# Hybrid attention layer on one core: block turns behind the weights, low halves on GpSimd, v through DRAM

## The chip, the cores and the metric

The kernel runs on one core of a Trainium2 chip. The core has TensorE (PE in the profile, with its weight loads as PEld), VectorE (DVE), ScalarE (ACT), GpSimd (POOL) and SyncE (SP), which here only issues DMA transfers. The metric is the device time in microseconds of one execution; several executions are timed and their median is given.

## The reference

One layer of an encoder trunk on 1024 frames of width 1024, with 16 meta tokens put ahead of them (1040 positions):

```python
u = rmsnorm(h, norm_g)
proj = einsum('bld,dc->blc', u, w_in)            # 1024 -> 4096 columns
sb_q, sb_k, sb_v, sb_g, df_q, df_k, df_v, df_g = split(proj)
# stick-breaking attention, 8 heads of 64, per block of 128 queries
z = q @ k.T * scale
log_keep = where(strict, log_sigmoid(-z), 0)
stick = reverse exclusive cumsum of log_keep along the keys
w = where(strict, exp(log_sigmoid(z) + stick), 0)
sb_o = w @ v
# differential attention, 4 heads, rotary, chunk-causal mask
a = softmax(s1) - lam * softmax(s2);  df_o = rmsnorm(a @ v) * (1 - lambda_init)
mix = concat([sb_o * silu(sb_g), df_o * silu(df_g)])
y = rmsnorm(h + mix @ w_out)[N_META:]
```

## The kernel before

**Numbers.** All is float32. The projections and q-times-k are done as products of two halves: a high half rounded to the short form in which TensorE is fast (float32r) and a low half that holds the rest. `mm3` (lines 150 to 160) makes three matmuls for each of the 8 slices of the contraction: high x high (L157), high x low (L158) and low x high (L159). `w_half` (line 140) loads half of a unit's weights (four slices of 128x128) from DRAM into `wraw` (L144, two buffers), ScalarE copies it to its high half `wh` (L146), and VectorE takes the difference as its low half `wl` (L147); `wh` and `wl` have three buffers each. There are 58 such halves outside the start: 8 for each of groups 1 to 7, and two for v of group 0.

**Stages.** The work has eight groups: 0 to 3 are pairs of stick-breaking heads (SB), 4 to 7 are heads of differential attention (DF). Each group has four projection units, q, k, v and gate. A weaver alternates the attention of group g with the projections of group g+1, by the costs that each piece states, so that TensorE has projection matmuls while VectorE and ScalarE work on weights. The framework's scheduler then sets the order of the instructions on each engine; each engine works through its own list in order, and so does SP's list of DMA transfers. A wait on one list holds up all that stands behind it there.

**SB attention.** The positions are stored in reverse, so block b of 128 queries has n = 8 - b key tiles behind it: 8, 7, 6, 5, 4, 3, 2, 1. `sb_attention` walks steps s = 0 to 8; step s makes the weights of block s and transposes those of block s-1, for both heads, and after every second block `sb_pv` multiplies the pair (b, b+1). `sb_weights` (line 512) does z on TensorE (L508, L509), a mask on VectorE (L520), two sigmoids on ScalarE (L521, L522), a running product on VectorE (TENSOR_TENSOR_SCAN, L525) and a product of weights (L527); GpSimd copies 16 columns of it aside (L528). The results lie in `be`, which has four buffers.

**Turning the weights.** The product with v needs the weights with keys on the partitions. `sb_transpose` (line 531) has two ways. With n of at least `SB_TURN` = 4 and b even (blocks 0, 2 and 4), and while the two rotary tables `cosr` and `sinr` aren't loaded yet (groups 0 to 2), `turn` (line 251) transposes blocks of 32x32 on VectorE (L256) into one of these two tables' room, writes the result to a scratch in DRAM with four transfers (L260) and reads it back whole (L262), at once, all in the step behind the weights. All other blocks are transposed by TensorE, 128x128 at a time (L551), and copied out of PSUM by ScalarE (L552). The results lie in `wt`, one tile for each head and pair of blocks, with two buffers: the next pair's tile is free when `sb_pv` (L574) has read the last pair's.

**v.** `make_v` (line 264) turns v of groups 1 to 6 in the same manner with VectorE (L279), but brings the pieces to their place with 16 transfers of 32 KB from SBUF to SBUF (L283), with runs of 128 bytes.

Of the kernel before, what the change touches and what calls it, by code (L numbers as in the profile page):

```python
# [52 lines left out]
class Build:  # L53
    def __init__(self, tc, es, i, out, mix_dram, turn_dram):
        self.tc, self.nc, self.es, self.i = tc, tc.nc, es, i
        self.out, self.mix_dram, self.turn_dram = out, mix_dram, turn_dram
        self.n = 0

        self.nu, self.rotary = 0, False

# [79 lines left out]
    def w_half(self, u, h, copy=None, room=None):  # L140
# [5 lines left out]
        (copy or nc.scalar.copy)(out=hi, in_=raw)  # L146
        nc.vector.tensor_sub(lo, raw, hi.bitcast(F32))  # L147
        return hi, lo
# [101 lines left out]

    def turn(self, u, src, dst):


        nc = self.nc
        n = src.shape[1] // P
        nc.vector.transpose(out=u[:, :n * P].rearrange("p (m t r) -> p t m r", m=4, r=32),  # L256
                            in_=src.rearrange("p (t m r) -> p t m r", m=4, r=32))
        d = self.turn_dram[self.nu % 4]
        for a in range(4):
            nc.sync.dma_start(out=d[:, a, :n * 32].rearrange("(m k) c -> k m c", k=32),  # L260
                              in_=u[32 * a:32 * a + 32, :n * P].rearrange("k (m c) -> k m c", m=4))
        nc.sync.dma_start(out=dst, in_=d[:, :, :n * 32].rearrange("p a (t r) -> p a t r", r=32))  # L262

    def make_v(self, t, st, sb, on_pe):
# [12 lines left out]
        else:  # L277
            u = self.tl(self.tp, [P, T], F32, "t")[:, :SEQ]
            nc.vector.transpose(out=u, in_=t[:, off:off + SEQ])  # L279
            u = u.rearrange("p (t j r) -> p t j r", j=4, r=32)  # L280
            for a in range(0, P, 32):
                for j in range(4):
                    nc.sync.dma_start(out=v[32 * j:32 * j + 32, :, a:a + 32], in_=u[a:a + 32, :, j, :])  # L283
        st["v"] = v
# [227 lines left out]
    def sb_weights(self, st, hd, b):  # L512
# [15 lines left out]
        nc.gpsimd.tensor_copy(st["wrem"][32 * hd:32 * hd + 16, b], beta[:16, :16])  # L528
        st["w", hd, b] = beta

    def sb_transpose(self, st, hd, b):
# [8 lines left out]
        wt = st["wt", hd][:, e]  # L540
        if e == 0 and n >= SB_TURN and not self.rotary:
            self.nu += 1
            u = self.tl(self.const, [P, T], F32, ("cosr", "sinr")[self.nu % 2])
            self.turn(u, w[:, NMETA:NMETA + n * P], wt[:, :, e:e + n])
            return
# [367 lines left out]

SB_TURN = 4

# [63 lines left out]
```

## Time and profile before

| what | value |
|---|---|
| median of 3 runs | 689.79 us (686.61 to 689.93) |
| the profiled execution | 689.24 us, span 687.4 us |
| PE busy | 663.5 us (97% of the span) |
| PEld busy | 577.5 us (84%) |
| DVE busy | 513.2 us (75%) |
| ACT busy | 350.8 us (51%) |
| POOL busy | 137.0 us (20%) |
| mean granted TensorE clock | 0.987 of full speed |
| DMA queues of SP | 76,416 packets, 78.10 MB, 41.6% of 16 engines' span |

The span runs from the first to the last instruction that the profile shows. The ends of matmuls are modelled, since they are pipelined: 0.40 us stands for a matmul that the next one follows after 0.23 us, so distances between starts tell more than durations. The granted clock is what the chip's throttle allowed TensorE, as a share of full speed. From its first z (L508) to the sum that ends it (L596), the attention of group 0 lies at 62 to 151 us of the span, of group 1 at 123 to 218, of group 2 at 201 to 292 and of group 3 at 273 to 368 (they overlap, since the next group's first z starts before the last products of the one before); then come the DF groups, and from about 560 us the output projection.

### The profile page before, as it was taken

What the parts mean: (1) busy time and instruction counts of PE and PEld (TensorE: products, weight loads), DVE (VectorE), ACT (ScalarE), POOL (GpSimd) and SP (SyncE); (2) the same over time, 40 slices, a digit from 0 to 9 for tenths busy, and PEclk for the clock granted to TensorE, in tenths of its full rate; (3) what the DMA queues carried; (4) which work ended last, traced back from release to release, by engine and by line L of the source; (5) the groups of instructions that cost most, each with busy time, mean ns of one, the idle gap of its engine ahead of it and who ended that gap; (6) DMA issues with size and microseconds to landing.
All of it is one profiled execution on the core that took longest, in us unless ns stands there. A gap on an engine that the chain in (4) does not pass through costs nothing.

```text
span 687.4 us, 11400 instructions
## 1 busy us (share of the span) xinstructions
PE 663.5 (97%) x3908; PEld 577.5 (84%) x3908; DVE 513.2 (75%) x1053; ACT 350.8 (51%) x931; POOL 137.0 (20%) x188
## 2 busy tenths in 40 slices
PE   8999999999979998989999999999999999999996
PEld 7888998798858996779878998899889987888785
DVE  6744998699829985698858785878589687776653
ACT  6513545545534552565544656555655436655642
POOL 0030021122210112040411022202222053011222
PEclk9999999999989999999999999999999999999998
DMA  8215647374645658022352324042504772122322
GB/s 327 93 33 140 171 124 188 87 218 121 144 118 138 165 112 239 16 77 55 72 123 62 74 67 124 32 117 53 124 32 101 201 239 87 63 84 77 105 92 92
DMA packets 76617, 78.83 MB, mean 115 GB/s; under 512 B 32528, under 2 KB 56208, under 8 KB 76560
## 3 DMA queue, kind: packets, MB, share of 16 engines
q1 hardware_dynamic: 76416, 78.10, 41.6%
q8 instruction: 31, 0.51, 0.3%
q14 instruction: 26, 0.21, 0.1%
q10 hardware_dynamic: 144, 0.00, 0.0%
HBM read 41.44 MB, written 14.42 MB: 81 GB/s over the span
## 4 chain that ended last, share of the span: by engine, by line
PE 71%; DVE 10%; DMA 8%; issue 3%; ACT 3%; SPq 3%; POOL 1%; POOLq 0%; DVEq 0%; ACTq 0%
PE mm L157 12%; PE mm L158 12%; PE mm L159 12%; PE mm L756 10%; PE pv L694 4%; PE z L508 4%; PE z L509 4%; PE pv L574 3%; DVE be L525 2%; PE tr L677 2%; DMA wt<-turn_scratch 2%; PE tr L551 2%; DVE be L527 1%; DMA hb<-ha 1%; SPq L283 1%
## 5 line engine op out<-in xcount | busy, mean ns | idle before, releaser
L157 PE MATMUL mm<-xh,wh 128*128 128x346 f32 (+2 forms) x592 | 211.6, 358 | 2.6 <-DVE be L211 2.2
L158 PE MATMUL mm<-xl,wh 128*128 128x346 f32 (+2 forms) x592 | 210.9, 356 | 0.0
L159 PE MATMUL mm<-xh,wl 128*128 128x346 f32 (+2 forms) x592 | 209.9, 355 | 0.0
L157 PEld LDWEIGHTS mm<-xh,wh 128*128 128x128 f32 x592 | 112.3, 190 | 13.3 <-DVE be L211 2.5
L159 PEld LDWEIGHTS mm<-xh,wl 128*128 128x128 f32 x592 | 112.1, 189 | 9.1 <-issue 0.5
L158 PEld LDWEIGHTS mm<-xl,wh 128*128 128x128 f32 x592 | 112.2, 189 | 8.5 <-issue 0.7
L525 DVE TENSOR_TENSOR_SCAN be<-be,zero 128x1040 f32<-128x1040 f32 (+7 forms) x64 | 92.2, 1446 | 16.5 <-ACT be L521 16.4
L521 ACT ACTIVATE be<-z 128x456 f32<-128x456 f32 (+8 forms) x112 | 49.8, 458 | 86.7 <-DVE z L520 51.2
L643 ACT ACTIVATE be<-z,nm 128x346 f32<-128x346 f32 (+8 forms) x112 | 59.9, 540 | 50.4 <-DVE nm L640 34.6
L528 POOL COPY rem<-be 16x16 f32<-16x16 f32 x64 | 34.6, 540 | 192.0 <-DVE be L527 177.0
L633 DVE TENSOR_REDUCE nm<-z 128x1 f32<-128x346 f32 (+8 forms) x112 | 54.6, 502 | 4.7 <-PE z L509 3.6
L522 ACT ACTIVATE be<-z 128x346 f32<-128x346 f32 (+8 forms) x112 | 48.6, 464 | 13.3 <-DVE be L527 12.1
L146 ACT CAST wh<-wraw 128x512 fp32r<-128x512 f32 x58 | 36.2, 626 | 36.6 <-PE mm L158 27.2
L527 DVE TENSOR_TENSOR be<-be,be 128x1039 f32<-128x1039 f32 (+7 forms) x64 | 49.2, 769 | 4.0 <-ACT be L522 0.9
L147 DVE TENSOR_TENSOR wl<-wraw,wh 128x512 fp32r<-128x512 f32 x58 | 40.0, 691 | 10.3 <-ACT wh L146 9.7
L702 POOL TENSOR_TENSOR rr<-rr,mhalf 128x1 f32<-128x1 f32 x32 | 19.7, 616 | 137.8 <-DVE rr L701 98.9
L508 PE MATMUL z<-ha,qa 128*128 128x346 f32 (+8 forms) x112 | 37.9, 344 | 4.2 <-DMA ha<-ha 1.9
L574 PE MATMUL pv<-wt,v 128*64 128x256 f32 (+1 forms) x336 | 37.4, 368 | 4.6 <-DMA wt<-turn_scratch 4.6
L508 PE MATMUL z<-hb,qb 128*128 128x346 f32 (+8 forms) x112 | 38.2, 341 | 0.6 <-ACT be L522 0.3
L552 ACT COPY wt<-tr 128x512 f32<-128x512 f32 (+3 forms) x66 | 28.7, 461 | 19.1 <-PE pv L574 9.5
L694 PEld LDWEIGHTS pv<-v,wt 128*128 128x128 f32 x288 | 36.8, 191 | 1.8
L694 PE MATMUL pv<-v,wt 128*128 128x128 f32 x288 | 38.2, 275 | 0.0
(237 smaller groups left out, 1220.1 us busy)
## 6 DMA issues: line engine op xcount, KB each, us to landing
wraw<-w_in SPq DMA_DIRECT2D x58, 256.0 KB, 3.0
t<-w_out SPq DMA_DIRECT2D x8, 512.0 KB, 4.3
wt<-turn_scratch SPq DMA_DIRECT2D x6, 512.0 KB, 4.4
v<-t SPq DMA_DIRECT2D x96, 32.0 KB, 2.0
mix_scratch<-gate SPq DMA_DIRECT2D x6, 512.0 KB, 4.0
t<-mix_scratch SPq DMA_DIRECT2D x16, 192.0 KB, 2.5
wt<-turn_scratch SPq DMA_DIRECT2D x6, 384.0 KB, 4.2
hb<-ha SPq DMA_DIRECT2D x8, 260.0 KB, 3.9
```

The costliest lines, as they stand in the source:

```text
L157: nc.tensor.matmul(o, hi[:, k, :], xh, start=kt == 0, stop=False)
L158: nc.tensor.matmul(o, hi[:, k, :], xl, start=False, stop=False)
L159: nc.tensor.matmul(o, lo[:, k, :], xh, start=False, stop=kt == KT - 1)
L508: nc.tensor.matmul(z[:, :cn], q, st["kh"][hd][:, s], start=True, stop=False)
L521: nc.scalar.activation(keep[:, c0:c0 + cn], z[:, :cn], AF.Sigmoid, scale=-1.0)
L525: nc.vector.tensor_tensor_scan(out=keep[:, :kw], data0=keep[:, :kw], data1=self.zero.to_broadcast([P, kw]), initial=1.0, op0=ALU.mult, op1 ...
L527: nc.vector.tensor_mul(beta[:, 1:kw], beta[:, 1:kw], keep[:, :kw - 1])
L574: nc.tensor.matmul(pv[r, s], st["v"][:, b + j, r], w, start=p in ends[0], stop=p in ends[1])
L633: nc.vector.tensor_reduce(out=nm[:, comp, j:j + 1], in_=z[:, :cn], op=ALU.max, axis=AX.X, negate=True)
L643: nc.scalar.activation(p[:, c0:c0 + cn], zs[j][:, :cn], AF.Exp, bias=bias, accum_out=sm[:, comp, j:j + 1])
L694: nc.tensor.matmul(po[:, :P], wt[:, m, :], st["v"][:, b + m, :], start=m == 0, stop=False)
L756: self.nc.tensor.matmul(ps[:, :cn], a, b[kt][:, w], start=first and n == 0, stop=last and n == 2)
```

## The change

Three things are changed. First, `sb_weights` now turns its block itself, right behind the product of weights, where n is at least 4 for even b and at least 5 for odd b (`SB_TURN = 4, 5`): blocks 0 to 4 in groups 0 to 2 instead of blocks 0, 2 and 4. `turn` does the transposition and the writes to DRAM and returns the read as a function; `sb_transpose` calls it a step later. The scratch in DRAM has 8 places instead of 4. Second, the low half of raw weights is taken by GpSimd instead of VectorE (L147). Third, `make_v` uses `turn` for v: four transfers to DRAM and four back, instead of 16 within SBUF.

```diff
--- before.py
+++ after.py
@@ -56,7 +56,7 @@
         self.out, self.mix_dram, self.turn_dram = out, mix_dram, turn_dram
         self.n = 0
 
-        self.nu, self.rotary = 0, False
+        self.nu, self.nd, self.rotary = 0, 0, False
 
     def name(self, s):
         self.n += 1
@@ -144,7 +144,7 @@
         nc.sync.dma_start(out=raw, in_=self.i["w_in"][u, :, 4 * h:4 * h + 4, :])
         hi, lo = room or (self.tl(self.wp3, [P, 4, P], F32R, n) for n in ("wh", "wl"))
         (copy or nc.scalar.copy)(out=hi, in_=raw)
-        nc.vector.tensor_sub(lo, raw, hi.bitcast(F32))
+        nc.gpsimd.tensor_sub(lo, raw, hi.bitcast(F32))
         return hi, lo
 
     def mm3(self, ps, w, kt, c0, cn):
@@ -248,18 +248,25 @@
                 self.move(a[r + n:r + 2 * n], a[r:r + n])
         st["kh"], st["kl"] = (ha, hb), (la, lb)
 
-    def turn(self, u, src, dst):
+    def turn(self, u, src):
+
 
 
         nc = self.nc
         n = src.shape[1] // P
         nc.vector.transpose(out=u[:, :n * P].rearrange("p (m t r) -> p t m r", m=4, r=32),
                             in_=src.rearrange("p (t m r) -> p t m r", m=4, r=32))
-        d = self.turn_dram[self.nu % 4]
+        self.nd += 1
+        d = self.turn_dram[self.nd % 8]
         for a in range(4):
             nc.sync.dma_start(out=d[:, a, :n * 32].rearrange("(m k) c -> k m c", k=32),
                               in_=u[32 * a:32 * a + 32, :n * P].rearrange("k (m c) -> k m c", m=4))
-        nc.sync.dma_start(out=dst, in_=d[:, :, :n * 32].rearrange("p a (t r) -> p a t r", r=32))
+        back = d[:, :, :n * 32].rearrange("p a (t r) -> p a t r", r=32)
+
+        def load(dst, by_a=False):
+            for a in (range(4) if by_a else [slice(0, 4)]):
+                nc.sync.dma_start(out=dst[:, a], in_=back[:, a])
+        return load
 
     def make_v(self, t, st, sb, on_pe):
 
@@ -276,11 +283,7 @@
                 nc.scalar.copy(out=v[:, j0:j0 + 4, :], in_=tr)
         else:
             u = self.tl(self.tp, [P, T], F32, "t")[:, :SEQ]
-            nc.vector.transpose(out=u, in_=t[:, off:off + SEQ])
-            u = u.rearrange("p (t j r) -> p t j r", j=4, r=32)
-            for a in range(0, P, 32):
-                for j in range(4):
-                    nc.sync.dma_start(out=v[32 * j:32 * j + 32, :, a:a + 32], in_=u[a:a + 32, :, j, :])
+            self.turn(u, t[:, off:off + SEQ])(v.rearrange("p t (a r) -> p a t r", a=4), by_a=True)
         st["v"] = v
         if sb:
             tc_ = self.tl(self.a3, [P, P], F32, "on")
@@ -526,7 +529,13 @@
                                      initial=1.0, op0=ALU.mult, op1=ALU.add)
         nc.vector.tensor_mul(beta[:, 1:kw], beta[:, 1:kw], keep[:, :kw - 1])
         nc.gpsimd.tensor_copy(st["wrem"][32 * hd:32 * hd + 16, b], beta[:16, :16])
-        st["w", hd, b] = beta
+        n = NB - b
+        if n >= SB_TURN[b % 2] and not self.rotary:
+            self.nu += 1
+            u = self.tl(self.const, [P, T], F32, ("cosr", "sinr")[self.nu % 2])
+            st["w", hd, b] = self.turn(u, beta[:, NMETA:NMETA + n * P])
+        else:
+            st["w", hd, b] = beta
 
     def sb_transpose(self, st, hd, b):
 
@@ -538,10 +547,8 @@
             wt = self.tl(self.a2, [P, 2 * NB * P], F32, "wt")
             st["wt", hd] = wt.rearrange("p (e a j r) -> p e a j r", e=2, a=4, r=32)
         wt = st["wt", hd][:, e]
-        if e == 0 and n >= SB_TURN and not self.rotary:
-            self.nu += 1
-            u = self.tl(self.const, [P, T], F32, ("cosr", "sinr")[self.nu % 2])
-            self.turn(u, w[:, NMETA:NMETA + n * P], wt[:, :, e:e + n])
+        if callable(w):
+            w(wt[:, :, e:e + n])
             return
         for m0 in range(0, n, 4):
             mn = min(4, n - m0)
@@ -911,7 +918,8 @@
 
 ORDER = [""] + 6 * ["qvrkg"] + ["qkvrg"]
 
-SB_TURN = 4
+
+SB_TURN = 4, 5
 
 AHEAD = 3
 LAST_CUT = [(0, 512), (512, 256), (768, 256)]
@@ -970,7 +978,7 @@
            for n, v in arrays.items()}
     out = nc.dram_tensor("out", (NB, P, D), F32, kind="ExternalOutput").ap()
     mix_dram = nc.dram_tensor("mix_scratch", (NB, P, KT, P), F32, kind="Internal").ap()
-    turn_dram = nc.dram_tensor("turn_scratch", (4, P, 4, NB * 32), F32, kind="Internal").ap()
+    turn_dram = nc.dram_tensor("turn_scratch", (8, P, 4, NB * 32), F32, kind="Internal").ap()
     with tile.TileContext(nc, **TC_OPTS) as tc:
         build(tc, ins, out, mix_dram, turn_dram)
     nc.finalize() if not nc.is_finalized() else None
```

Where the instructions now stand, at three places. VectorE, at blocks 1 and 2 of group 2 (L525 and L528 are the running product before and after the change, L527 and L530 the product of weights, L256 and L257 the turn). Before:

```order
L525 SCALAR_TENSOR_TENSOR be_2233<-be_2233,zero 128x912
L199 TENSOR_TENSOR t_2152<-mm_2246,rstd_b 128x512
L527 TENSOR_TENSOR be_2232<-be_2232,be_2233 128x911
L147 TENSOR_TENSOR wl_2569<-wraw_2566,wh_2568 128x512
L225 SCALAR_TENSOR_TENSOR t_2325<-t_2152,qa_2323 128x1024
L520 TENSOR_TENSOR z_2308<-z_2308,zmask 128x128
L525 SCALAR_TENSOR_TENSOR be_2268<-be_2268,zero 128x912
```

With the change:

```order
L528 SCALAR_TENSOR_TENSOR be_2199<-be_2199,zero 128x912
L601 TENSOR_TENSOR grem_1341<-pv_2081,grem_1341 128x128
L530 TENSOR_TENSOR be_2198<-be_2198,be_2199 128x911
L603 TENSOR_TENSOR gate_1183<-gate_1183,grem_1341 128x8x16
L225 SCALAR_TENSOR_TENSOR t_2287<-t_2112,qa_2285 128x1024
L257 STREAM_TRANSPOSE sinr_2225<-be_2198 128x7x4x32
L528 SCALAR_TENSOR_TENSOR be_2234<-be_2234,zero 128x912
```

The subtraction L147 is gone from this list, and the turn of block 1 (7 tiles) stands three rows behind its product of weights. VectorE has 30 turns of weights instead of 18 in all, 10 in each of groups 0 to 2, and 6 of v in both kernels.

GpSimd, in group 1 (`rem` receives the 16 columns of each block's weights, L528 before and L531 after). Before:

```order
L528 COPY rem_1363<-be_1747 16x16
L528 COPY rem_1363<-be_1827 16x16
L528 COPY rem_1363<-be_1891 16x16
L528 COPY rem_1363<-be_1927 16x16
L528 COPY rem_1363<-be_1958 16x16
```

With the change:

```order
L531 COPY rem_1343<-be_1679 16x16
L147 TENSOR_TENSOR wl_1952<-wraw_1949,wh_1951 128x512
L531 COPY rem_1343<-be_1717 16x16
L147 TENSOR_TENSOR wl_2116<-wraw_2113,wh_2115 128x512
L531 COPY rem_1343<-be_1787 16x16
L531 COPY rem_1343<-be_1851 16x16
L531 COPY rem_1343<-be_1879 16x16
L531 COPY rem_1343<-be_1912 16x16
L147 TENSOR_TENSOR wl_2122<-wraw_2119,wh_2121 128x512
```

Each low half now stands between copies that wait for VectorE's products of weights.

SP, in group 1, between the reads of turned weights for blocks 2 and 3 and those for block 4 (`wt<-turn_scratch`: L262 before, L268 after; the writes: L260 before, L262 after; hb, lb, ha and la are the moves that stack the next group's k). Before:

```order
L260 DMA turn_scratch<-sinr_1884 32x4x128 x4
L260 DMA turn_scratch<-cosr_1920 32x4x128 x4
L144 DMA wraw_2159<-w_in 128x512
L144 DMA wraw_2332<-w_in 128x512
L216 DMA hb_1971<-ha_1970 64x1040 x2
L216 DMA lb_1973<-la_1972 64x1040
L262 DMA wt_1883<-turn_scratch 128x4x128
L262 DMA wt_1919<-turn_scratch 128x4x128
```

With the change:

```order
L268 DMA wt_1677<-turn_scratch 128x4x160
L262 DMA turn_scratch<-cosr_1818 32x4x128 x4
L216 DMA hb_1931<-ha_1930 64x1040 x2
L216 DMA lb_1933<-la_1932 64x1040 x2
L144 DMA wraw_2119<-w_in 128x512
L216 DMA ha_1930<-ha_1930 64x1040
L144 DMA wraw_2294<-w_in 128x512
L216 DMA la_1932<-la_1932 64x1040
L268 DMA wt_1849<-turn_scratch 128x4x128
L268 DMA wt_1877<-turn_scratch 128x4x128
```

Block 3 is now read from DRAM too (its row is the first), and all moves of the next group's k stand ahead of the reads for block 4, where three of them stood before. In all SP issues 452 transfers instead of 440.

## Rows read from the trace of the kernel before

**Rows 1.** The page, part 1: busy us (share of the span) and instructions of each engine.

```profile
PE 663.5 (97%) x3908; PEld 577.5 (84%) x3908; DVE 513.2 (75%) x1053; ACT 350.8 (51%) x931; POOL 137.0 (20%) x188
```

**Rows 2.** Stretches: us, busy PE, PEld, DVE, ACT, POOL (instructions), PEclk, DMA share, GB/s.

```profile
150.00:182.00 32.00, 31.83 (x223) 28.23 (x221) 31.49 (x45) 18.01 (x45) 8.28 (x11) 1.00 0.54 136
182.00:206.00 24.00, 19.63 (x98) 14.52 (x96) 9.84 (x20) 8.25 (x23) 4.33 (x7) 0.86 0.55 145
206.00:256.00 50.00, 50.00 (x321) 44.53 (x322) 47.16 (x65) 25.09 (x61) 6.80 (x15) 1.00 0.57 139
```

**Rows 3.** PE in order of time, 186 to 195: start, duration, instruction [idle before it <-releaser].

```profile
188.05 0.40 PE L158 MATMUL mm<-xl,wh 128*128 128x512 f32 x1
188.29 0.40 PE L159 MATMUL mm<-xh,wl 128*128 128x512 f32 x1
...
193.28 1.97 PE L574 MATMUL pv<-wt,v 128*64 128x256 f32 x10 [4.37 <-DMA wt<-turn_scratch]
```

**Rows 4.** SP's DMA issues in order of time, 178 to 196.

```profile
179.16 2.00 SPq L260 DMA_DIRECT2D turn_scratch<-sinr  x4
...
186.80 2.87 SPq L262 DMA_DIRECT2D wt<-turn_scratch  x2
```

**Rows 5.** The stretch behind the gap, columns as in rows 2.

```profile
194.00:200.00 6.00, 6.00 (x27) 4.12 (x24) 1.81 (x5) 1.64 (x5) 0.00 (x0) 0.65 0.24 52
```

**Rows 6.** PE in order of time at seven transposes of group 0, 84.5 to 87.

```profile
85.03 0.93 PE L551 MATMUL tr<-ident,be 128*128 128x128 f32 x7
85.71 0.40 PE L159 MATMUL mm<-xh,wl 128*128 128x348 f32 x1
85.95 0.32 PE L157 MATMUL mm<-xh,wh 128*128 128x348 f32 x1
86.10 0.32 PE L158 MATMUL mm<-xl,wh 128*128 128x348 f32 x1
```

**Rows 7.** Groups of instructions by shape: count | busy us, mean ns | idle before, releaser.

```profile
L256 DVE STREAM_TRANSPOSE sinr<-be 128x1024 f32<-128x1024 f32 x3 | 3.7, 1243 | 0.1
L256 DVE STREAM_TRANSPOSE sinr<-be 128x512 f32<-128x512 f32 x3 | 2.1, 705 | 0.0
L147 DVE TENSOR_TENSOR wl<-wraw,wh 128x512 fp32r<-128x512 f32 x58 | 40.0, 691 | 10.3 <-ACT wh L146 9.7 <-PE pv L697 0.3
L325 POOL TENSOR_TENSOR gate<-gate,be 128x512 f32<-128x512 f32 x16 | 21.3, 1342 | 31.4 <-ACT be L322 26.6 <-DVE cc L653 4.3 <-POOL rem L528 0.6
```

**Rows 8.** L147 alone in 150 to 182 and 206 to 256: both together.

```profile
sum 82.00, DVE 6.30; mean DVE 3.15
```

**Rows 9.** DVE, then POOL, then PE in order of time, 292 to 306.

```profile
293.75 2.93 DVE L525 TENSOR_TENSOR_SCAN be<-be,zero 128x912 f32<-128x912 f32 x1
...
299.00 2.04 DVE L525 TENSOR_TENSOR_SCAN be<-be,zero 128x912 f32<-128x912 f32 x1
...
303.71 2.68 DVE L525 TENSOR_TENSOR_SCAN be<-be,zero 128x784 f32<-128x784 f32 x1
...
293.47 1.30 POOL L212 TENSOR_TENSOR t<-t,be 128x512 f32<-128x512 f32 x1 [1.29 <-DVE be L211]
...
304.81 1.57 POOL L528 COPY rem<-be 16x16 f32<-16x16 f32 x1
...
302.51 0.42 PE L157 MATMUL mm<-xh,wh 128*128 128x346 f32 x1 [2.18 <-DVE be L211]
```

**Rows 10.** DVE and PE in order of time: a low half, and the first matmul that reads it.

```profile
157.46 0.68 DVE L147 TENSOR_TENSOR wl<-wraw,wh 128x512 fp32r<-128x512 f32 x1
...
159.68 0.32 PE L159 MATMUL mm<-xh,wl 128*128 128x348 f32 x1
```

**Rows 11.** Issues of v on SP (ns, min/median/max); the page, part 6 (KB each, us to landing).

```profile
L283 SPq DMA_DIRECT2D v<-t x96: 591/609/1377, 90.2 to 470.4; - x96
...
wt<-turn_scratch SPq DMA_DIRECT2D x6, 384.0 KB, 4.2
```

**Rows 12.** The chain that ended last, in order of time: start, us, what.

```profile
179.21 2.53 PE pv L574 x24
```

## The prediction

> **What bounds the kernel now.** I read the busy times first. TensorE (PE) is busy for 663.5 of 687.4 us, VectorE (DVE) for 513.2, ScalarE for 350.8 and GpSimd (POOL) for 137.0 [rows 1]. PE has only 24 us without work, so time is won by giving PE fewer instructions or by closing those gaps. A mean hides the stages, so I read stretches next [rows 2]. While the large blocks of groups 1 and 2 are weighted, VectorE is as full as PE: 31.49 of 32 us in 150 to 182, and 47.16 of 50 us in 206 to 256. Together it has 3.35 us left there. Behind them, in 182 to 206, VectorE works for 9.84 of 24 us. So PE and VectorE are both at their end early in a group, PE alone late in it.
>
> The third view is PE's order of time at the largest gap [rows 3]. The weight-times-v product (L574) of blocks 4 and 5 of group 1 starts at 193.28, 4.37 us after PE ran dry, and the releaser is the load of turned weights from DRAM. SyncE's (SP) own rows show why: it is at the writes of these turns from 179.16 on, has moves and raw weights behind them, and issues the two loads only from 186.80 on [rows 4]. The gap costs more than itself: the granted clock is 1.00 in 150 to 182 and 0.65 in 194 to 200 [rows 2, 5], a mean of the two levels of 2.4 and 1.2 GHz. 0.35 x 6 us = 2.1 us go there, so the gap costs about 6.5 us in all.
>
> **The change part by part.** The sum is made against the profiled execution's own time, 689.24 us (span 687.4); the median of the three runs is 689.79, 0.55 higher, so the two may be read as one.
>
> *Transposes leave PE.* In groups 0, 1 and 2, both heads of blocks 1 (7 tiles) and 3 (5 tiles) are turned elsewhere: 3 x 2 x 12 = 72 transposes. Group 3 keeps its own, because the rotary tables then hold the two turning buffers. Seven transposes start at 85.03; the next matmul comes at 85.71 and the one behind it at 85.95, 0.24 us later, where the next pair of this shape stands 0.15 apart [rows 6]. That is 0.68 + 0.09 = 0.77 us, or 0.11 each. 72 x 0.11 = **-7.9 us**, all on the path, since PE is the end nearly everywhere. With them go 24 copies out of PSUM (L552); ScalarE is half idle [rows 1], so nothing for these.
>
> *Transposes come to VectorE.* A turn costs it 1.243 us for 8 tiles and 0.705 for 4 [rows 7], so 0.1345 per tile: 1.11 for 7, 0.84 for 5. Per group 2 x 1.95 = 3.9 us are added. Since every turn now stands straight behind its weights, the weights' buffer (`be`, four of them) comes free a step earlier.
>
> *Low halves leave VectorE.* 58 subtractions (L147) of 691 ns are 40.0 us [rows 7], 8 to a group. In the two full stretches they take 6.3 us, about nine of them [rows 8], while the turns add 7.8 there: +1.5 us, hidden by the 3.35 us that VectorE has left.
>
> *Low halves come to GpSimd.* The nearest row is the gate's product on GpSimd (L325), also 128x512 from two operands: 1342 ns [rows 7]. 58 x 1.34 = 78 us make GpSimd busy for 215 of 687 us, far from a bound. What is not free is the room beside VectorE [rows 9]. A product on GpSimd runs from 293.47 to 294.77; a VectorE scan over 912 elements that starts in it takes 2.93 us, where the same shape takes 2.04 alone. In the other direction, a copy of 16 by 16 on GpSimd starts at 304.81 and ends at 306.38, as the scan of 303.71 does. So the two engines shut each other out there. Call h what one low half on GpSimd holds VectorE up by: between 0 (VectorE is reading PSUM at that moment) and 0.9 us. Nine of them stand in the two full stretches. VectorE then needs 1.5 + 9h there and has 3.35: -1.85 + 9h is late. I take h = 0.4, near the middle, since part of VectorE's work between scans reads PSUM: 1.75 us, and one fall of the clock of 2.1 with it: **+4 us** (bounds 0 and, at h = 0.9 with two falls, 6.25 + 4.2 = +10.5). That such lateness reaches PE is seen at 302.51, where it had waited 2.18 us for VectorE right behind that long scan [rows 9].
>
> The Trainium skill speaks against this part: "GPSIMD Engine Reference", section "Key points", says that GpSimd shares its SBUF interfaces with VectorE and contends with VectorE's instructions that have two SBUF inputs. The trace agrees, with 2.93 against 2.04 us. By that rule every scan and every product of weights collides, and h would be at its upper end: that is the first rival below.
>
> *A low half that comes later.* In place of 0.69 it takes 1.34 us, and it now queues on GpSimd behind copies that wait for VectorE (the order on GpSimd in the part on the change). The first matmul that reads a low half shows the slack: the half that ended at 158.14 (start 157.46) was read at 159.68, 1.54 us later [rows 10]. 0.65 more fits even there; a wait for a scan on top does not. **+1 us** (bounds 0 and 4).
>
> *v by way of DRAM.* 96 issues of 609 ns on SP go (9.7 us for each v) [rows 11]; 24 writes and 24 loads come. The turns add 12 x 5 = 60 issues, so SP issues 452 in place of 440. v is read by the next group only, so its own time is hidden; if that cover were gone, it would cost PE about one load of 4.2 us [rows 11].
>
> *The wait at 188.* By the changed order, SP reaches the loads for block 4 of group 1 behind four writes, six moves and two raw loads after the last load for block 3. That is 12 x about 0.6 = 7.2 us, 0.6 for the load itself, and 4.2 to land [rows 11]: 12.0 us. PE can start the product of blocks 2 and 3 when that last load of theirs has landed (4.2), spends 2.5 us on it [rows 12], and by the order has 22 matmuls of 512 columns before the next product, 0.23 us apart [rows 3], 5.1 us, with ten transposes of 0.11, 1.1 us: 12.9. So PE just covers it, if nothing on SP waits. Between the whole gain of 6.5 and none I take the middle: **-3 us**.
>
> Sum: 689.24 - 7.9 + 4 + 1 - 3 = 683.3, forecast **683 us**. Groups 4 to 7 are left as they are: their low halves move too, but there VectorE mostly reads PSUM and is not the end.
>
> **The rivals.** *VectorE is held up as much as it can be.* h = 0.9 for all nine low halves in the full stretches, and two falls of the clock: +10.5 in place of +4, so 689.8; with the wait at 188 unchanged 692.8. For it: both meetings in [rows 9] show a full hold-up. Against it: VectorE also spends time on sums and evictions from PSUM, beside which GpSimd is free. It gives no change that can be told.
>
> *Slower: the loads of turned weights come late in every group.* The place is the product of blocks 4 and 5 (L574 before), whose loads may go out only when the product of blocks 2 and 3 has given its buffer back. Before, one of three groups waited there. Now 12 issues stand between the loads of one pair and the next, and moves among them wait for other moves. It decides from 0.9 us of such waits on: beyond that PE is dry, and with 4.37 us, as at 188, each gap costs 6.5 with the clock. Two more of them and the old one kept: 689.24 - 7.9 + 4 + 1 + 13 = 699.3 us. For it: the sum above leaves 12.9 against 12.0. Against it: SP loses eight issues of v ahead of that place.
>
> *Faster than forecast.* The wait at 188 goes wholly and VectorE stays within its 3.35 us: 689.24 - 7.9 - 6.5 = 674.8.
>
> *The change does less than it says.* If PE's freed time only becomes idle time because VectorE sets the pace of the full stretches of groups 1 and 2, two thirds of 7.9 us are worth nothing: 683.3 + 5.3 = 688.6. This falls into the same bin as the first rival.
>
> **How the numbers follow.** A measurement of this kernel can tell about 0.5% from no change, 3.4 us: faster means below 686.3, slower above 693.2. The forecast and what lies around it, 677 to 686.3: 0.44. The faster case: 0.08. No change, from the first and the last rival, 688 to 693: 0.26. Slower, from the loads (0.14) and from the first rival together with late low halves (0.08): 0.22. So faster 0.52, same 0.26, slower 0.22. The range has to take in the faster case and the first rival whole and reaches to the slower one: 675 to 698. The likeliest case's own range is 677 to 687.
>
> **What would show it.** Right: PE without the 72 transposes, its matmul order some 8 us shorter; VectorE's subtractions gone and 30 turns in place of 18; low halves of about 1.3 us on GpSimd, longer where a scan runs; no gap of 4 us ahead of the weight-times-v products. Each step wrong: scans of VectorE that take 0.9 us more each time a low half runs (h too small); PE waiting for GpSimd at the third matmul of a half (slack too small); PE waiting for `wt<-turn_scratch` in several groups, with the clock below 1.00 behind it (the slower rival). The prediction as a whole is wrong if the time stays above 686.3, and the first thing to look at then is VectorE's mean scan time.

## The result, and the profile after

The changed kernel takes **709.12 us** (median of 4 runs, 706.36 to 712.5), the kernel before 689.39 on the same chip: 1.0278 times as long, with a 95% interval of 1.0239 to 1.0317. It is slower by about 19.7 us, where 683.0 was forecast, with a range of 675 to 698. The profiled execution took 706.36 us, with a span of 704.6.

The first part of the page of the changed kernel, busy time, share and instructions, which answers to [rows 1]:

```profile
PE 662.2 (94%) x3836; PEld 576.6 (82%) x3836; DVE 507.9 (72%) x1007; ACT 343.1 (49%) x907; POOL 211.2 (30%) x246
```

PE has 72 instructions fewer, as the change says, but its busy time falls by 1.3 us only and it stands idle for 42.4 us in place of 23.9. To see where, the span is cut into six stretches, of which the four inner ones are shown. The view by stretches of the kernel before (PE, PEld, DVE, ACT and POOL busy with their instructions, then the granted clock, DMA share and GB/s):

```profile
60.00:200.00 140.00, 134.38 (x815) 115.43 (x814) 111.67 (x159) 67.34 (x164) 24.41 (x38) 0.98 0.57 144
200.00:360.00 160.00, 154.24 (x928) 130.50 (x926) 127.28 (x188) 80.86 (x191) 33.83 (x50) 0.98 0.43 110
360.00:500.00 140.00, 138.62 (x859) 126.66 (x859) 104.80 (x291) 78.93 (x235) 25.95 (x30) 1.00 0.32 80
500.00:640.00 140.00, 137.93 (x804) 120.91 (x803) 110.51 (x308) 78.25 (x254) 34.70 (x45) 1.00 0.37 115
```

The same stretches of the changed kernel:

```profile
60.00:200.00 140.00, 130.10 (x759) 114.32 (x757) 113.69 (x147) 59.68 (x142) 38.88 (x50) 0.98 0.73 192
200.00:360.00 160.00, 145.86 (x866) 121.45 (x867) 123.57 (x172) 75.93 (x178) 55.78 (x68) 0.97 0.53 136
360.00:500.00 140.00, 138.29 (x855) 125.52 (x854) 100.32 (x274) 76.36 (x231) 42.89 (x46) 1.00 0.35 88
500.00:640.00 140.00, 133.57 (x762) 117.69 (x761) 103.14 (x278) 76.21 (x238) 42.63 (x48) 0.98 0.34 105
```

Two places lose. In 60 to 360, the stick-breaking groups, PE is idle for 24.0 us in place of 11.4 (300 minus the two busy times). In 500 to 640, where the last projection ends and the output begins, it is 6.4 in place of 2.1. The 140 us between are as before. VectorE is busy for 113.69 of 140 us and 123.57 of 160 in the first two, but that is a mean: in 150 to 182 it is at 30.36 of 32 us. That it is not the end there either is shown only by a run further down, in which it does more (120.19 of 140 us) and PE hardly waits.

What PE waited for in the changed kernel (us in all, times, longest):

```profile
PE pv L581 <- DMA wt<-turn_scratch: 10.5, 5, 4.0
PE z L511 <- ACT be L650: 3.6, 3, 1.6
PE mm L763 <- DVE gate L320: 3.1, 1, 3.1
PE z L511 <- DMA ha<-ha: 2.5, 1, 2.5
PE tr L558 <- DVE be L530: 2.4, 2, 1.7
...
PE mm L159 <- POOL wl L147: 1.5, 1, 1.5
```

The first row read before:

```profile
PE pv L574 <- DMA wt<-turn_scratch: 4.6, 2, 4.4
```

The third row is new. The loads of turned weights are now late at three of the products that hold a second block turned in the new way: 4.04 us at 119.20 (blocks 2 and 3 of group 0), 3.10 at 173.50 and 1.80 at 245.64 (blocks 0 and 1 of groups 1 and 2). The old wait of [rows 3], at blocks 4 and 5 of group 1, shrank to 0.75:

```profile
203.03 1.33 PE L581 MATMUL pv<-wt,v 128*64 128x256 f32 x6 [0.75 <-DMA wt<-turn_scratch]
```

One of these waits from end to end. The turn of block 1 on VectorE, then SP's issues, then PE (in each row start, duration, line, and for PE the idle time before it):

```profile
160.25 1.09 DVE L257 STREAM_TRANSPOSE cosr<-be 128x896 f32<-128x896 f32 x1
...
161.98 0.57 SPq L268 DMA_DIRECT2D wt<-turn_scratch  x1
162.65 0.56 SPq L144 DMA_DIRECT2D wraw<-w_in  x1
163.31 1.89 SPq L262 DMA_DIRECT2D turn_scratch<-cosr  x4
165.24 0.85 SPq L144 DMA_DIRECT2D wraw<-w_in  x1
166.14 1.99 SPq L262 DMA_DIRECT2D turn_scratch<-sinr  x4
168.23 0.57 SPq L268 DMA_DIRECT2D wt<-turn_scratch  x1
...
173.50 0.74 PE L581 MATMUL pv<-wt,v 128*64 128x256 f32 x5 [3.10 <-DMA wt<-turn_scratch]
```

The turned block is ready at 161.34. SP had issued nothing since 158.49: it stood at the load of 161.98, which stands ahead in its list. So it takes up this turn's writes 1.97 us after the turn, has another raw load and the next turn's four writes behind them, and issues the load at 168.23; the product starts 13.25 us after the turn began. A second block's weights are finished only one step ahead of its pair's product, and PE's work of that step ended at 170.4.

### The profile page after: what moved, and what is told of

Same layout as the page of the kernel before. It is cut to its first block, busy times and chain, and to the rows that moved or that the text cites. A ratio compares the mean times of both kernels' runs of the same rounds, so it can differ in the third digit from the quotient of the medians.

```text
span 704.6 us, 11293 instructions
## 1 busy us (share of the span) xinstructions
PE 662.2 (94%) x3836; PEld 576.6 (82%) x3836; DVE 507.9 (72%) x1007; ACT 343.1 (49%) x907; POOL 211.2 (30%) x246
## 4 chain that ended last, share of the span: by engine, by line
PE 70%; DMA 10%; DVE 10%; ACT 3%; SPq 3%; issue 2%; POOL 1%; POOLq 0%; DVEq 0%; ACTq 0%
PE mm L157 12%; PE mm L159 12%; PE mm L158 12%; PE mm L763 11%; PE pv L581 5%; DMA wt<-turn_scratch 4%; PE pv L701 4%; PE z L511 4%; PE z L512 3%; PE tr L684 2%; SPq L262 2%; DMA turn_scratch<-cosr 2%; DVE be L528 1%; PE tr L558 1%; DVE be L530 1%
## 5 line engine op out<-in xcount | busy, mean ns | idle before, releaser
L147 POOL TENSOR_TENSOR wl<-wraw,wh 128x512 fp32r<-128x512 f32 x58 | 85.9, 1483 | 124.9 <-ACT wh L146 112.4
L528 DVE TENSOR_TENSOR_SCAN be<-be,zero 128x1040 f32<-128x1040 f32 (+7 forms) x64 | 95.1, 1492 | 16.6 <-ACT be L524 16.5
L524 ACT ACTIVATE be<-z 128x346 f32<-128x346 f32 (+8 forms) x112 | 49.9, 456 | 89.0 <-DVE z L523 56.6
L530 DVE TENSOR_TENSOR be<-be,be 128x1039 f32<-128x1039 f32 (+7 forms) x64 | 56.4, 881 | 7.4 <-ACT be L525 4.9
L531 POOL COPY rem<-be 16x16 f32<-16x16 f32 x64 | 25.7, 402 | 118.8 <-DVE be L530 117.3
L525 ACT ACTIVATE be<-z 128x346 f32<-128x346 f32 (+8 forms) x112 | 48.5, 460 | 17.2 <-DVE be L530 7.5
L581 PE MATMUL pv<-wt,v 128*64 128x256 f32 (+1 forms) x336 | 40.7, 388 | 10.7 <-DMA wt<-turn_scratch 10.5
L581 PEld LDWEIGHTS pv<-wt,v 128*64 128x64 f32 x336 | 27.7, 150 | 21.8 <-issue 14.8
```

The lines of the kernel that those rows point to most:

```text
L147: nc.gpsimd.tensor_sub(lo, raw, hi.bitcast(F32))
L528: nc.vector.tensor_tensor_scan(out=keep[:, :kw], data0=keep[:, :kw], data1=self.zero.to_broadcast([P, kw]), initial=1.0, op0=ALU.mult, op1 ...
L530: nc.vector.tensor_mul(beta[:, 1:kw], beta[:, 1:kw], keep[:, :kw - 1])
L581: nc.tensor.matmul(pv[r, s], st["v"][:, b + j, r], w, start=p in ends[0], stop=p in ends[1])
```

## The experiments

Each run is timed beside the kernel before on the same chip; a ratio is to that kernel, with its 95% interval. "L147 back" means that the line reads as in the kernel before.

### One part at a time

**Only the low halves** (kernel before):

```diff
-        nc.vector.tensor_sub(lo, raw, hi.bitcast(F32))
+        nc.gpsimd.tensor_sub(lo, raw, hi.bitcast(F32))
```

> The kernel before, with only the low halves moved to GpSimd. Theory L (the low halves are the loss: GpSimd takes 1.48 us for one, so the raw buffers come free late, SP stands longer at the raw loads, and GpSimd and VectorE hold each other up): most of the 19.7 us appear here, so 700 to 709 us. Theory T (the loads of turned weights are late, 5 waits of PE and 10.5 us, in DMA engines filled by turns and v): 686 to 693, no change. Theory R (each edit makes the scheduler write another order, and the order at the end of group 7 is the loss): anything from 685 to 700, with gaps on PE behind other releasers than in the changed kernel.

Measured: 704.36 us, 1.0197 (1.0153 to 1.0241).

**Only v by way of DRAM** (kernel before):

```diff
-            for a in range(0, P, 32):
-                for j in range(4):
-                    nc.sync.dma_start(out=v[32 * j:32 * j + 32, :, a:a + 32], in_=u[a:a + 32, :, j, :])
+            for a in range(4):
+                nc.sync.dma_start(out=d[:, a, :].rearrange("(m k) c -> k m c", k=32), in_=...)
+            for a in range(4):
+                nc.sync.dma_start(out=v.rearrange("p t (a r) -> p a t r", a=4)[:, a], in_=...)
```

> The kernel before, with only v turned by way of DRAM (8 DMAs for each v in place of 16). Theory L: 688 to 691. Theory T: 690 to 696, since the round trip puts 8 more transfers per group beside the loads of turned weights. Theory R: 685 to 700, and not explained by v.

Measured: 686.87 us, 0.9953 (0.9928 to 0.9978). It helps a little.

**Only the turns** (the changed kernel with L147 and `make_v` back):

> The kernel before, with only the blocks: second blocks of 7 and 5 tiles turned by VectorE, all turns straight behind the weights; v and low halves as before. Theory L: the 7.9 us of transposes show and VectorE pays for the turns, 683 to 690. Theory T: 697 to 706, with PE waiting for the loads of turned weights as in the changed kernel (10.5 us). Theory R: 685 to 700.

Measured: 711.08 us, 1.0302 (1.0256 to 1.0348). The turns alone cost as much as the whole change.

**All but the low halves** (the changed kernel with L147 back):

> The changed kernel with the low halves back on VectorE. Theory L: 686 to 692, most of the loss is gone. Theory T: 702 to 710, the loss stays. Theory R: 690 to 705, with the gap of 3.10 us at the start of the output part gone or elsewhere.

Measured: 700.96 us, 1.0147 (1.0098 to 1.0196). It lies between the theories: there are two losses, the turns and the low halves, and they don't add up: 20.4 and 13.7 us alone, less v's 3.8, would be 30.3, and the change cost 19.7.

### The turns: place, number, or SP's list

**The old 18 turns, straight behind their weights** (as "only the turns", but even blocks alone):

```diff
-SB_TURN = 4, 5
+SB_TURN = 4, 99
```

> The kernel before, with the old 18 turns only, but each straight behind its weights; second blocks stay on TensorE, v and low halves as before. If the place of the turns is the loss (VectorE stands at the next turn until the writes out of one of the two turning buffers have landed, and holds up what is queued behind it): 698 to 710, as with all turns (711.1). If the number of turns is the loss: 686 to 693. If only the scheduler's order is: 685 to 700, whatever the place.

Measured: 687.72 us, 0.9984 (0.9956 to 1.0013). This does not show that the place costs nothing, since the place did not change: in the traces of this run and of the kernel before, PE, VectorE, ScalarE and GpSimd run the same instructions in the same order, and only SP's list differs a little. The 18 old turns already stood where this edit wants them.

**All 30 turns, where turns were before** (L147 and `make_v` back):

```diff
-            st["w", hd, b] = self.turn(u, beta[:, NMETA:NMETA + n * P])
+            st["w", hd, b] = beta
...
-        if callable(w):
-            w(wt[:, :, e:e + n])
+        if n >= SB_TURN[e] and not self.rotary:
+            self.turn(u, w[:, NMETA:NMETA + n * P])(wt[:, :, e:e + n])
```

> The kernel before, with the second blocks of 7 and 5 tiles turned by VectorE as well, but all turns where they were, at the block's transposes; v and low halves as before. Place is the loss: 683 to 691, the transposes' 7.9 us shows at least in part. Number is the loss (loads that come only when the product needs them, 12 more turns through DRAM): 697 to 712.

Measured: 714.25 us, 1.0374 (1.0313 to 1.0436). Here the order on VectorE does differ from that of "only the turns", and 30 turns lose in either place, so it is their number that costs. PE's waits between 60 and 360 show that not only turned weights are late:

```profile
PE z L515 <- DMA ha<-ha: 11.8, 2, 7.1
PE pv L582 <- issue: 5.3, 1, 5.3
PE pv L582 <- DMA wt<-turn_scratch: 4.4, 1, 4.4
```

The longest of them, in order of time: ScalarE's copy that makes `ha`, SP's list behind it (the row of v at 271.35 is ten issues), and PE's first z of the next group:

```profile
264.88 1.06 ACT L242 CAST ha<-t 128x1040 fp32r<-128x1040 f32 x1
...
271.35 6.55 SPq L290 DMA_DIRECT2D v<-t  x10
278.00 2.02 SPq L262 DMA_DIRECT2D turn_scratch<-cosr  x4
280.12 0.90 SPq L262 DMA_DIRECT2D turn_scratch<-sinr  x2
281.49 0.58 SPq L268 DMA_DIRECT2D wt<-turn_scratch  x1
282.11 1.14 SPq L262 DMA_DIRECT2D turn_scratch<-sinr  x2
283.30 1.93 SPq L262 DMA_DIRECT2D turn_scratch<-cosr  x4
285.32 1.17 SPq L216 DMA_DIRECT2D hb<-ha  x2
...
296.33 1.23 PE L515 MATMUL z<-ha,qa 128*128 128x348 f32 x3 [7.11 <-DMA ha<-ha]
```

`ha` is ready at 265.94, and SP first moves it at 285.32, 19.4 us later: v and turns stand ahead of it in the list. This would explain that v by way of DRAM, with 8 issues in place of 16, helps more beside 30 turns (711.1 to 701.0) than alone (690.7 to 686.9): in "only the turns" PE waits 5.8 us for `ha`, in "all but the low halves" not at all. It was not tried apart.

**The writes of the turns issued by GpSimd** (on "all but the low halves"):

```diff
-            nc.sync.dma_start(out=d[:, a, :n * 32].rearrange(...
+            nc.gpsimd.dma_start(out=d[:, a, :n * 32].rearrange(...
```

> The changed kernel with low halves on VectorE (701.0 with SP), the writes of the turns into DRAM now issued by GpSimd, which is idle for 80% there; so SP loses 144 issues and its waits for VectorE's turns. If SP's order is what makes the loads of turned weights late: 684 to 694 and PE's waits for them shrink from 7.6 us to under 4. If the transfers themselves are late (DMA engines full): 699 to 706.

Measured: 690.23 us, 0.9999 (0.9972 to 1.0027), so 10.7 us come back, with the same turns and the same bytes. The stretch from 60 to 200 in the run that it is based on, with all issues on SP:

```profile
60.00:200.00 140.00, 127.05 (x737) 110.44 (x737) 114.75 (x156) 58.89 (x138) 15.84 (x33) 1.00 0.72 189
```

And with the writes on GpSimd:

```profile
60.00:200.00 140.00, 138.03 (x804) 120.85 (x803) 120.19 (x169) 62.32 (x146) 67.39 (x126) 1.00 0.71 201
```

PE is idle for 2.0 us of 140, against 13.0, at the same DMA share (0.71 and 0.72), and its waits for turned weights in this stretch fall from 7.6 us to 0.2. Over the whole kernel they fall to 5.5 us only, not under the 4 expected: two products of group 2 still wait. So the DMA engines, though fuller than before (0.57), are not what was late. The writes also changed to a queue of GpSimd's own, but the loads did not land sooner for it: 4.4 us from issue to landing (median between 60 and 280) against 4.1. What changed is when they are issued. This run still loses 12.8 us between 200 and 360. Counted from SP's rows between 60 and 280, SP issues for 111 us in the kernel before, 127 in the changed one and 61 here.

**The raw weights issued by GpSimd instead** (on "all but the low halves"):

```diff
-        nc.sync.dma_start(out=raw, in_=self.i["w_in"][u, :, 4 * h:4 * h + 4, :])
+        nc.gpsimd.dma_start(out=raw, in_=self.i["w_in"][u, :, 4 * h:4 * h + 4, :])
```

> The changed kernel with low halves on VectorE (701.0), the raw weights' loads issued by GpSimd, turns and v on SP as they were. If SP's time is lost where it stands at a raw load that waits for its buffer, with loads of turned weights behind it: 686 to 693, as good as the writes on GpSimd. If it is lost where it stands at a write that waits for VectorE's turn: 698 to 704.

Measured: 705.92 us, 1.0239 (1.0209 to 1.027). Nothing is won; it is slower than its base (1.0147). SP's standing at raw loads, 40 us between 60 and 280, is gone with it and the time does not come back, which speaks against the wait for raw buffers. But it takes only 25 issues from SP there, where the writes are 132, so it leaves open whether SP's count of issues or its standing at writes weighs more. In the run that both are based on, SP spends 72 us there on issuing the writes and some 19 us standing at them. The order is not held fixed either: with the writes on GpSimd the scheduler puts the product of blocks 0 and 1 of group 1 16.8 us behind the last turn's start, in place of 12.9.

### The low halves: early groups, late groups

**Low halves of groups 0 to 3 alone on GpSimd** (kernel before):

```diff
-        nc.vector.tensor_sub(lo, raw, hi.bitcast(F32))
+        (nc.vector if self.rotary else nc.gpsimd).tensor_sub(lo, raw, hi.bitcast(F32))
```

> The kernel before, with low halves on GpSimd for the parts that project groups 1 to 3 and the first of group 4, and on VectorE from the rotary tables on. The run with all of them on GpSimd took 704.4, with 4.8 us more of PE's idle time behind 560 us. If that end is a loss of the low halves of group 7 (the gate's eviction stands on VectorE behind halves of w_out): 696 to 699, and the gap before the first output matmul is gone. If the loss all comes from the early groups: 702 to 706.

Measured: 692.39 us, 1.0043 (1.0017 to 1.0069). So of the 13.7 us that all low halves cost alone, some 2 belong to these 26, and the rest to those of groups 4 to 7.

**Low halves of group 7 alone on GpSimd** (kernel before):

```diff
+        (nc.gpsimd if u > 15 and u % 4 == 3 else nc.vector).tensor_sub(lo, raw, hi.bitcast(F32))
```

> The kernel before, with the eight low halves of group 7 alone on GpSimd. All 58 there took 704.4, those of the early groups alone 692.4, so some 12 us belong to groups 4 to 7. If it is the end (on VectorE the eviction of the last gates stands behind halves of w_out that wait for GpSimd; PE waits 3.5 us for it and the clock falls): 695 to 703, with a wait of PE for the gate's eviction before the first output matmul. If it is groups 4 to 6: 688 to 693.

Measured: 693.9 us, 1.0066 (1.0046 to 1.0087): less than expected from the end, but its mark is there. Its waits:

```profile
PE pv L574 <- DMA wt<-turn_scratch: 7.1, 3, 5.2
PE mm L756 <- DVE gate L317: 3.2, 1, 3.2
```

**The changed kernel with the low halves of groups 4 to 7 back on VectorE** (the same line of code as for groups 0 to 3):

> The changed kernel, with low halves back on VectorE from the rotary tables on (groups 4 to 7); the early ones stay on GpSimd. The sum of the parts: the end costs some 4 to 12 us, so 697 to 705, and the wait of 3.10 us for the gate's eviction before the first output matmul goes. If the end is not a loss of its own: 707 to 711.

Measured: 700.16 us, 1.0152 (1.0121 to 1.0183). 9 us come back and the wait for the gate's eviction is gone. So roughly half of the change's loss came with halves of which the prediction had said that they change nothing. PE's idle time shrinks by 4.4 us in 500 to 640, and by 2.5 already in 200 to 360, where group 4's halves are made. In the changed kernel the place at the end looks so (VectorE, then PE):

```profile
570.96 2.10 DVE L193 TENSOR_TENSOR xl<-t,xh 128x512 fp32r<-128x512 f32 x2 [0.51 <-POOL xh L191]
...
573.53 0.69 DVE L193 TENSOR_TENSOR xl<-t,xh 128x512 fp32r<-128x512 f32 x1
...
575.00 0.68 DVE L193 TENSOR_TENSOR xl<-t,xh 128x512 fp32r<-128x512 f32 x1
...
576.02 1.28 DVE L320 TENSOR_TENSOR gate<-mm,rstd_b 128x512 f32<-128x512 f32 x2
...
576.86 0.47 PE L763 MATMUL mm<-xh,cosr 128*128 128x512 f32 x1 [3.10 <-DVE gate L320]
```

PE's last gate matmul starts at 571.48. The eviction that frees its PSUM banks stands on VectorE behind halves of `w_out` (L193), which wait for GpSimd's copies (L191), and comes at 576.02; before, the two evictions stood among those halves and PE never waited for them:

```profile
561.99 0.68 DVE L317 TENSOR_TENSOR gate<-mm,rstd_b 128x512 f32<-128x512 f32 x1
...
563.19 0.68 DVE L317 TENSOR_TENSOR gate<-mm,rstd_b 128x512 f32<-128x512 f32 x1
```

In the changed kernel the granted clock is 0.66 in 577 to 582.

### A control, and the parts put together

**One constant of the plan, 2% more** (kernel before, no work moved):

```diff
-SB_PAD, DF_PAD = 5000, 3000
+SB_PAD, DF_PAD = 5100, 3000
```

> A control: the kernel before with one constant of the plan changed by 2% (SB_PAD 5100 in place of 5000), which moves no work to another engine and only shifts how attention and projection are woven. If the order alone can cost what the parts of the change cost: 695 to 710. If order is worth a few us: 686 to 694.

Measured: 690.6 us, 1.0007 (0.9984 to 1.003). This new order is worth nothing that can be told; it is one order, and does not bound what others cost.

**The changed kernel with the turns' writes on GpSimd and the late low halves on VectorE:**

> The changed kernel with two edits: the turns' writes issued by GpSimd, and the low halves back on VectorE from the rotary tables on. If the loss is SP's queue (10.7 us by the pair 701.0 and 690.2) and the low halves of groups 4 to 7 (12), and the early low halves cost about 2: 688 to 694. If GpSimd, with low halves and 144 issues, becomes what SP was: 697 to 706.

Measured: 717.1 us, 1.0404 (1.037 to 1.0438), the slowest of all. GpSimd then has low halves and writes in one list in the same groups, and PE waits 9.2 us, 8 times, for ScalarE's sigmoids. In this run, low halves and DMA issues on GpSimd don't go together.

**First blocks only, early, v by DRAM, writes on GpSimd, low halves on VectorE:**

> What the parts point to: first blocks alone turned, straight behind their weights, v by way of DRAM (686.9 alone), the turns' writes issued by GpSimd, low halves on VectorE. If SP's queue also made the one wait of 4.4 us in the kernel before: 678 to 685. If the 18 turns were served well enough by SP: 685 to 690. If the issues on GpSimd cost VectorE or late releases: 690 to 697.

Measured: 690.55 us, 1.0023 (1.0 to 1.0046). With 18 turns, taking the writes off SP brings nothing; beside the next run, which differs in the writes alone, it costs some 0.5%.

**The same with all DMAs on SP:**

> First blocks alone turned, straight behind their weights, v by way of DRAM, all DMAs on SP, low halves on VectorE. v alone gave 686.9, the place alone 687.7, each with 690 beside it: if they add, 682 to 686; if the wait at the loads of turned weights stays as it is (6.0 us in the run with v alone): 685 to 689.

Measured: 687.81 us, 0.9975 (0.9958 to 0.9992). As above, the place did not change: all engines but SP run the same instructions in the same order as with v alone. So this is v alone once more, and its gain is 0.25 to 0.5%.

**As with the writes on GpSimd, second blocks turned in groups 0 and 1 only:**

```diff
+        st["lim"] = SB_TURN if gi < 2 else (4, 99)
...
-        if n >= SB_TURN[b % 2] and not self.rotary:
+        if n >= st["lim"][b % 2] and not self.rotary:
```

> As the run with the turns' writes issued by GpSimd (690.2), but second blocks turned by VectorE only in groups 0 and 1. In that run PE lost 2.0 us of idle time in 60 to 200 and 12.8 with 7.4 of clock in 200 to 360, around the loads of the rotary tables into the turning buffers. If the turns of group 2 cause the latter: 679 to 685 (2.6 us of transposes come back to PE). If not: 688 to 694.

Measured: 686.62 us, 0.9953 (0.9935 to 0.997). PE's waits for turned weights are down to 2.2 us. The largest that is left (VectorE, ScalarE, PE):

```profile
282.77 0.22 DVE L129 TENSOR_TENSOR be<-be 128x64 f32<-128x64 f32 x1 [4.28 <-DMA be<-lambda_k]
...
284.44 0.81 ACT L525 ACTIVATE be<-z 128x348 f32<-128x348 f32 x2 [4.69 <-DVE be L129]
...
284.95 0.75 PE L511 MATMUL z<-ha,qa 128*128 128x456 f32 x1 [4.95 <-ACT be L525]
```

The four lambda vectors, a few hundred numbers, take one of the four `be` buffers; VectorE stands at them until their loads land, the sigmoids stand for the buffer, and PE for the sigmoids.

**That, with the lambda vectors at the start of the kernel** (the lines from `lam = ...` to `nlam` go from `df_constants` to the end of `late_constants`):

> e12_odd_two_groups (686.6) with the four lambda vectors loaded and multiplied at the start of the kernel. If the wait of 4.95 us and the clock's 2.2 us around it come from the buffer that they hold: 678 to 682, and no wait of PE over 2 us between 280 and 300. If another wait takes its place: 684 to 688.

Measured: **682.31 us**, 0.9908 (0.988 to 0.9936), faster than both kernels, with no wait of PE for turned weights among its longest rows:

```profile
PE mm L157 <- DVE t L199: 3.2, 3, 2.2
PE tr L558 <- DVE be L530: 2.1, 3, 1.3
PE pv L598 <- DVE gate L583: 1.7, 1, 1.7
```

**v alone with the lambda vectors at the start:**

> v alone by way of DRAM (686.9), with the lambda vectors at the start of the kernel. PE loses 4.4 us between 280 and 360 there, none of it behind the lambda vectors: 685 to 688, no gain. If the constants are worth as much here: 680 to 684, and the turns have no part in the gain of e16_lambda_early.

Measured: 684.02 us, 0.992 (0.9899 to 0.9942). v alone gave 0.9953 and, once more, 0.9975. So the constants are worth some 2 to 4 us here as well, clear of noise against the second of these only. The intervals of the last two runs overlap: they don't show that 8 more turns a kernel bring anything beyond v by DRAM and the constants' place.

## Why the prediction was wrong

Two steps failed: the wait at 188, which was balanced for one place alone, and the sentence that leaves groups 4 to 7 out of the sum. Step by step:

*Transposes leave PE.* Right in its number: 180 of them became 108, 3908 PE instructions became 3836. The price of 0.11 each was too high: summed over both traces, from start to next start without idle time, the transposes of weights take 5.6 us less, about 0.08 for each of the 72. The products of turned weights and v take 3.3 us more: the one behind the gap at 119.20 runs at a granted clock of 0.51. PE's idle time grew by 18.5 us.

*Transposes come to VectorE.* Right in the price: 1.08 to 1.11 us for 7 tiles against 1.11. That every turn now stands earlier is not so for the 18 old ones: moved by themselves, they keep the order that they had.

*Low halves come to GpSimd.* The hold-up was near what was taken, and the cost lay elsewhere. VectorE's scans and products of weights in the kernel before, then the rows of the changed kernel with the low halves that answer to [rows 7]:

```profile
L525 DVE TENSOR_TENSOR_SCAN be<-be,zero 128x1040 f32<-128x1040 f32 (+7 forms) x64 | 92.2, 1446 | 16.5 <-ACT be L521 16.4
L527 DVE TENSOR_TENSOR be<-be,be 128x1039 f32<-128x1039 f32 (+7 forms) x64 | 49.2, 769 | 4.0 <-ACT be L522 0.9
...
L147 POOL TENSOR_TENSOR wl<-wraw,wh 128x512 fp32r<-128x512 f32 x58 | 85.9, 1483 | 124.9 <-ACT wh L146 112.4 <-DMA turn_scratch<-sinr 5.4 <-ACT be L524 3.6
L528 DVE TENSOR_TENSOR_SCAN be<-be,zero 128x1040 f32<-128x1040 f32 (+7 forms) x64 | 95.1, 1492 | 16.6 <-ACT be L524 16.5
L530 DVE TENSOR_TENSOR be<-be,be 128x1039 f32<-128x1039 f32 (+7 forms) x64 | 56.4, 881 | 7.4 <-ACT be L525 4.9
```

So VectorE was held up by 2.9 + 7.2 = 10.1 us, while 40.0 us left it. With the low halves back on VectorE and all else changed, scans and products take 93.6 and 48.7 us, so about 9.2 us of this are the low halves' doing. Only 31 of the 58 run while there are scans and products (64.8 to 359.7 us), so h is about 0.3, near the 0.4 taken, and the first rival (h = 0.9) is out. What the early halves cost as a whole is less than the +5 of this step and the next: 1.9 us in the run that has them alone on GpSimd. The reading of [rows 9] at 302.51 does not hold as it is put: the scan straight ahead of that wait, at 299.00, took the 2.04 us of a scan alone, and the long one had ended at 296.68. The Trainium skill's "GPSIMD Engine Reference", section "Key points", is borne out in kind, and more for the products, which read two arrays, than for the scans; the size is the runs'. What failed is the sentence "Groups 4 to 7 are left as they are": 9 us of the loss come with their halves, by the run that takes just those back, and the wait seen there is not a hold-up of VectorE but one for an eviction that stands late in its list. Why the evictions come to stand behind the halves of `w_out` was not tried apart; the mark of it (3.1 to 3.5 us for the gate) is in the runs that have group 7's low halves on GpSimd, and missing from those that have them on VectorE.

*A low half that comes later.* Right: one wait, 1.5 us, against +1.

*v by way of DRAM.* Taken as 0; alone it gained 0.25 to 0.5%, at the edge of what can be told, and beside the turns 10 us. SP's time had a price that the step did not see.

*The wait at 188.* The old wait did go, from 4.37 to 0.75, and "PE just covers it, if nothing on SP waits" held for that place. The step that failed is that the balance of 12.0 against 12.9 us was struck for that place alone. A second block's turn must come back within one step, and that was not worked out for blocks 0 to 3: 160.25 to 173.50 is 13.25 us, and PE was dry for the last 3.10. -3 was forecast; the waits for turned weights went from 4.6 to 10.5 us.

*The rivals.* The slower one, "loads of turned weights come late in every group", named the right mechanism, priced it at 699.3, and had the place wrong (blocks 4 and 5 rather than the pairs with a new turn). It also had no term for the late low halves, 9 us. Its chance of 0.14 was too low: the prediction counted SP's issues over the whole kernel (452 for 440), while between 60 and 280 the count went from 198 to 228 and the time from 111 to 127 us of 220.

What stays open: how much of SP's loss is its count and how much its standing at a write, and what all of the 5 us are that separate the cost of the late low halves (9) from that of group 7's alone (3.9). A part is seen at group 4: between 280 and 360, PE is idle for 5.7 us in the run with the low halves alone on GpSimd, and for 2.4 where only the early ones are there.

## What to carry to other kernels

Work that moves from an engine to a round trip through DRAM moves onto the list that issues the transfers: count the issues of the stretch in which they fall, not of the kernel, and look at what else stands in that list: with all 30 turns in the old place, late moves of k cost PE 11.8 us and late weights 4.4. For every value that now takes the round trip, set its time from producer to consumer (13 us here) against the work in between, place by place. And a part that moves to another engine in all groups must be priced in all groups: nearly half of this loss came with groups whose turns no one had touched, the largest wait of it at the end of the kernel.

## What the runs showed that was not expected

DMA share is no measure of a late transfer: 0.72 and 0.71 in 60 to 200, with 13.0 and 2.0 us of idle PE. The Trainium skill's "DMA: Bandwidth & Descriptors", section "Issuing engines are not separate DMA queues", says that issuing from several engines saves only the time to start transfers, usually small beside the transfer. The runs agree in that the DMA share stays the same, and show when that time is not small: with 132 writes between 60 and 280 on SP, 72 us of issuing, taking them off was worth 10.7 us.

A low half takes 1483 ns on GpSimd on the mean, where the gate's product that stood for it takes 1342; the 22 behind 360 us, where no scan runs, take 1337, and those before it 1571. GpSimd's busy share, 30% of the span, told nothing of either loss.
